# A new order for projection and router, 19 ring slots with six early weight halves, and a pool for the memory keys that closes with attention

## The chip, the cores and the metric

The kernel runs on one NeuronCore of a Trainium2 chip. The metric is the device time of one execution in microseconds; the median of three executions of the kernel before is 940.51 us (937.72 to 942.25). Engines: PE is TensorE's matmul, PEld its weight load, DVE is VectorE, ACT is ScalarE, POOL is GpSimd, SP is SyncE, which issues nearly all loads here.

## The reference

One decoder layer on 512 tokens of width 1024. Three attention branches (block-sparse, stick-breaking, and cross-attention into 256 memory tokens) share one projection; their gated sum goes through an output projection; two layer norms stand around the residual; then each token picks one of four groups and two of the eight experts in it.

```python
proj = x @ w_in
...
merged = (gates[:, :, 0] * (y_a @ w_br_moba)
          + gates[:, :, 1] * (y_b @ w_br_sb)
          + gates[:, :, 2] * (y_m @ w_br_mem))
mix = merged @ w_out
x = layer_norm(ALPHA * x + mix)          # norm 1
...
e_in_group = e_logits[top group]         # router
top_l, top_i = lax.top_k(e_in_group, 2)
gate = g_p * jax.nn.softmax(top_l)
...
h = jax.nn.silu(xb @ w_gate[e]) * (xb @ w_up[e])
y = h @ w_down[e]                        # 32 experts, 1024 -> 512 -> 1024
x = layer_norm(ALPHA * x + combined)     # norm 2
```

## The kernel before

The work runs in stages. First all projections, the attention of the three branches and the gates, with every fp32 matmul split into three rounded ones (`mm3`, L122). Then the output projection of the merged branches: its first four K-tiles are added up on the way (`add_out`), the last four are kept (`wo`, L581) and are done by `project(t)` (L824), t being one of four blocks of 128 tokens. `project` does 24 matmuls of 128x512: two column halves, K-tiles 0 to 2 first, then K-tile 3, which needs `mg[7]`, the last merged block. It adds the result to x1, norms the block (`norm`, L596) and sends it to DRAM. `turn_x` (T) transposes a normed block, `route` (L) computes router logits and the two picked experts (`ab`), `place` (R) ranks the block's tokens among all before it (`rank`) and builds the selection matrix `sel`, and `gather0` (A) gathers the block's tokens for the first pair of experts. ORDER (L48) is the list in which TensorE executes these steps; TensorE follows it to the letter, whereas VectorE, ScalarE and GpSimd are ordered by a planner that prefers, among what it holds for ready, what was emitted first.

Then 16 pairs of experts, `pair_step(p)`: gate (two halves of K), combine of the pair before, up (two halves), hidden, transposes, down (two halves of columns). A weight half is 128x2048 fp32, 1 MB; a pair has 12, there are 192. They are loaded by `fetch` (L528) into a ring of 18 slots (`ring`, L517): RB = 4 in `ring2`, which is there right after attention, RA = 9 in `ring1` (after the projections), RC = 4 in `ring3` and RD = 1 in `ring4` (after the router); two more go into a tile "once", used in pair 0 alone. A slot is allocated in a fixed rotation over the four pools, so a half waits until its pool has a slot given back. `ahead(n)` issues n halves; 4 are issued during the projections (two when ct is 2, two when ct is 4), 20 in all ahead of pair 0.

After pair 0 stands a loop with a bound known only at run time (the overflow of experts with over 64 tokens, L1158), which all engines enter and leave together. Ahead of it `ahead(BEFORE)` issues six more halves; the halves behind it can't be issued until the loop is left. The rest of the kernel runs over pairs 1 to 15, and `last` (L1108) does the last pair's down projection, the combine and norm 2, all engines in the order written. There `inner(t, i)` applies mean and gain to a block of 128x512 on VectorE, `outer(t, i)` the deviation and offset, by TensorE and ScalarE, or by VectorE for the blocks in BYDVE, and `ship` stores it.

Of the kernel before, what the change touches and what calls it, by code (L numbers as in the profile page):

```python
# [11 lines left out]
F32 = mybir.dt.float32  # L12
F32R = mybir.dt.float32r
# [4 lines left out]
ALU = mybir.AluOpType  # L18
# [4 lines left out]
P = 128  # L23
S = 512
D = 1024
KT = D // P
TT = S // P
# [6 lines left out]
WB, LOOK = 2, 1  # L34
F_M, F_A, F_B = 3.9, 3.9, 3.9
H = (slice(0, 64), slice(64, 128))
RA, RB, RC, RD = 9, 4, 4, 1
HALF = 2048
MIDP = 0
BEFORE = 6  # L40
CW = 184
BIG = 8192.0
XTB = 2
HTB = 1
BYDVE = ((3, 0), (3, 1))
BANKS = ("ht", "gu", "dn", "cb", "xgp", "cb", "", "")
FIRST = (2, 1)
ORDER = "G0 G1 T0 G2 L0 T1 G30 L1 R0 G31 A0 T2 L2 T3 R1 L3 R2 A1 R3 A2 A3"  # L48


@with_exitstack
def layer(ctx, tc, xT, xn, memT, w_qk, w_v, w_mk, w_mv, w_g, w_o, rb, oh, ln, wr, br,
# [34 lines left out]
    astk = ExitStack()  # L87
# [2 lines left out]
    xl = xp.tile([P, KT, S], F32R, name="xl")  # L90
    yh = yp.tile([P, KT, S], F32R, name="yh")
    yl = yp.tile([P, KT, S], F32R, name="yl")
    vm = xp.tile([P, 2, 256], F32, name="vm")
    km = [[xp.tile([P, 256], F32R, name=f"km{i}{j}") for j in range(2)] for i in range(2)]
    identb = cpool.tile([P, P], BF16, name="identb")
    ve.tensor_copy(identb, ident)
    maskb = cpool.tile([P, P], BF16, name="maskb")
# [24 lines left out]
    def mm3(o, pairs, start=True, stop=True):  # L122
        n = len(pairs)
        for i, (lh, ll, rh, rl) in enumerate(pairs):
            pe.matmul(o, lh, rh, start=start and i == 0, stop=False)  # L125
            pe.matmul(o, ll, rh, start=False, stop=False)  # L126
            pe.matmul(o, lh, rl, start=False, stop=stop and i == n - 1)  # L127
# [421 lines left out]

    todo = [x for p in range(16) for x in pieces_of(p)]  # L550

    todo[4:15] = todo[4:6] + todo[8:15] + todo[6:8]
    taken = [0]

    def ahead(n, ts=()):

        for i in range(n):
            e, j, c = todo[taken[0]]
            taken[0] += 1
            pieces[e, j, c] = fetch(e, j, c, ts[i] if i < len(ts) else None)  # L560
# [5 lines left out]
    for ct in range(6):  # L566
        jobs.finish(f"br{ct}")
        if ct == 3:
            lastw[0] = jobs.last
            for i in range(2):  # L570
                after(nc.sync.dma_start(lnb[:, i, :], ln[i:i + 1, :].to_broadcast([P, D])), lastw[0])
            after(nc.sync.dma_start(wrt, wr), lastw[0])
            after(nc.sync.dma_start(brt, br.to_broadcast([P, 40])), lastw[0])
        if ct in (2, 4):
            lastw[0] = jobs.last
            ahead(2)
    jobs.finish("g23")
    jobs.load(len(jobs.jobs) - 1)
    xstk.close()
# [7 lines left out]
    def bank3(tag):  # L587
        return ps.tile([P, 512], F32, name=tag, tag=tag, bufs={"gu": 2, "dn": 2, "xgp": 1, "ht": 1, "cb": 2}[tag])
# [1 line left out]
    half = cpool.tile([P, 1], F32, name="half")  # L590
    ve.memset(half, -0.5)

    rw = op.tile([P, TT, 96], F32, name="rw")
    sm = op.tile([P, TT, 8], F32, name="sm")

    def norm(t, sm, gb, sp):  # L596
# [18 lines left out]
    rpool = ctx.enter_context(pool("rout", waits="tile"))  # L615
    gpool2 = ctx.enter_context(pool("slots", waits="tile"))

    cs = rpool.tile([P, CW], F32, name="cs")
    nc.sync.dma_start(cs, cst[:, 0:CW])
    nc.sync.dma_start(cs2, cst[:, CW:CW + 160])  # L620
# [200 lines left out]
    pairs[0].start()  # L821
    first = []

    def project(t, cols=(0, 1)):  # L824

        ts = slice(t * P, (t + 1) * P)
        os_ = [bank3("dn") for c in cols]
        for ks in (range(3), range(3, 4)):
            for c, o in zip(cols, os_):
                r = slice(c * 512, (c + 1) * 512)  # L830
                mm3(o, [(mg[4 + k][0][:, ts], mg[4 + k][1][:, ts], wo[k][0][:, r], wo[k][1][:, r]) for k in ks],
                    start=ks[0] == 0, stop=ks[0] == 3)
        for c, o in zip(cols, os_):
            r = slice(c * 512, (c + 1) * 512)
            ve.scalar_tensor_tensor(out=x1[:, t, r], in0=x1[:, t, r], scalar=1.0, in1=o, op0=ALU.mult, op1=ALU.add,
                                    accum_out=sm[:, t, c:c + 1])
        if 1 in cols:
            norm(t, sm, lnb, op)
            gp.dma_start(xdr[ts, :], x1[:, t, :])
# [10 lines left out]
    with tc.manual_schedule(engines={mybir.EngineType.PE}):  # L850
        xt_ = {}
        for step in ORDER.split():
            t = int(step[1])
            if step[0] == "G":
                project(t, (0, 1) if len(step) == 2 else (int(step[2]),))
                if t == 0:
                    first += [bank3("xgp"), bank3("cb")]
            elif step[0] == "T":
                xt_[t] = turn_x(t)
            elif step[0] == "L":  # L860
                route(t, xt_[t])
            elif step[0] == "R":
                place(t)
            else:
                gather0(t)
        settle()
# [179 lines left out]
    def last_norm(gb):  # L1046

        col = lambda i: slice(i * 512, (i + 1) * 512)

        def inner(t, i):  # L1050
            x = x1[:, t, col(i)]
            ve.scalar_tensor_tensor(out=x, in0=x, scalar=sm2[:, t, 5:6], in1=gb[:, 0, col(i)], op0=ALU.add, op1=ALU.mult)  # L1052

        def ship(t, i):
            nc.sync.dma_start(out[t * P:(t + 1) * P, col(i)], x1[:, t, col(i)])

        m, d = sm2[:, :, 5], sm2[:, :, 6]
        ve.tensor_tensor(out=m, in0=sm2[:, :, 0], in1=sm2[:, :, 1], op=ALU.add)
        ve.tensor_scalar(out=m, in0=m, scalar1=-1.0 / D, scalar2=None, op0=ALU.mult)
        ve.scalar_tensor_tensor(out=d, in0=sm2[:, :, 0], scalar=2.0 / D, in1=m, op0=ALU.mult, op1=ALU.add)  # L1060
        ve.tensor_tensor(out=d, in0=d, in1=d, op=ALU.mult)
        inner(0, 0)

        v = [sm2[:, :, i] for i in range(8)]
        ve.scalar_tensor_tensor(out=v[3], in0=v[3], scalar=EPS * D ** 3 / 4.0, in1=v[4], op0=ALU.add, op1=ALU.add)
        ve.scalar_tensor_tensor(out=v[3], in0=v[3], scalar=4.0 / D ** 3, in1=v[6], op0=ALU.mult, op1=ALU.subtract)
        gp.tensor_tensor(out=v[7], in0=v[3], in1=half.to_broadcast([P, TT]), op=ALU.pow)
        inner(0, 1)
        inner(1, 0)
        diag = late[0].tile([P, TT, P], F32, name="diag", tag="hT", bufs=1)  # L1070

        def spread(ts):
            ve.tensor_tensor(out=diag[:, ts, :], in0=ident.unsqueeze(1).to_broadcast([P, ts.stop - ts.start, P]),
                             in1=v[7][:, ts].unsqueeze(2).to_broadcast([P, ts.stop - ts.start, P]), op=ALU.mult)

        def outer(t, i):
            x = x1[:, t, col(i)]
            if (t, i) in BYDVE:
                ve.scalar_tensor_tensor(out=x, in0=x, scalar=v[7][:, t:t + 1], in1=gb[:, 1, col(i)], op0=ALU.mult, op1=ALU.add)
            else:  # L1080
                pe.matmul(os_[t, i], diag[:, t, :], x, start=False, stop=True)  # L1081
                sc.copy(x, os_[t, i])
            ship(t, i)

        inner(1, 1)
        spread(slice(0, 2))
        for t in range(2):
            outer(t, 0)
            outer(t, 1)
        inner(2, 0)  # L1090
        spread(slice(2, 4))
        outer(2, 0)
        inner(2, 1)
        outer(2, 1)
        inner(3, 0)
        inner(3, 1)
        outer(3, 0)
        outer(3, 1)

    os_ = {}  # L1100

    def offset(gb, a, b):

        for n in range(a, b):
            os_[n // 2, n % 2] = o = bank3(BANKS[n])
            pe.matmul(o, ident, gb[:, 1, n % 2 * 512:n % 2 * 512 + 512], start=True, stop=False)

    def last(hT):  # L1108
        pair = pairs[15]
        b = [None, None]  # L1110

        def part(c, ks):
            if ks[0] == 0:
                pair.room(c)
                b[c] = bank3("dn")
                held[:] = [weights(30 + q, 2, c) for q in range(2)]
            for k in ks:
                for q in range(2):
                    pe.matmul(b[c][H[q]], hT[:, k, H[q]], held[q][:, k * 512:(k + 1) * 512], start=k == 0, stop=k == 3)  # L1119

        part(0, range(4))
        pair.out = b[0]
        pair.finish(0)
        part(1, range(2))
        lnt = ring().rearrange("p (a b) -> p a b", b=D)
        for i in range(2):
            nc.sync.dma_start(lnt[:, i, :], ln[2 + i:3 + i, :].to_broadcast([P, D]))
        last_sums(0, ("cb", "xgp", "gu", "cb"))
        part(1, range(2, 4))
        ve.tensor_copy(pair.y_h[1], b[1])  # L1130
        ve.tensor_tensor(out=pair.y_l[1], in0=b[1], in1=pair.y_h[1].bitcast(F32), op=ALU.subtract)
        offset(lnt, 0, 2)
        last_sums(1, ("cb", "xgp", "gu", "cb"))
        offset(lnt, 2, 6)
        last_norm(lnt)

    hTs = []
# [20 lines left out]
    with tc.For_i(0, nov, 1) as i:  # L1158
# [13 lines left out]
        ve.tensor_copy(pair.si[0:64, 0:1], sp[0:64, 0:1])  # L1172
        ve.tensor_copy(pair.si[0:64, 2:3], sp[0:64, 1:2])
        pair.rows(64)
        pair.xg = late[0].tile([P, KT, 64], F32, name="xg_o")
        o = bank3("xgp")
        for k in range(KT):
            pe.transpose(o[:, k * 64:(k + 1) * 64], xrow[0][0:64, k * P:(k + 1) * P], ident[0:64, 0:64])
# [120 lines left out]
```

## Time and profile before

| | us |
|---|---|
| median of three executions | 940.51 |
| the profiled execution, its own time | 942.12 |
| its span, first to last instruction | 940.3 |
| PE busy | 896.4 (95%) |
| DVE busy | 454.3 (48%) |
| ACT busy | 261.8 (28%) |
| DMA, mean rate over the span | 272 GB/s, 255.58 MB |

Busy time of TensorE counts from a matmul's issue to its modelled end, so a busy TensorE isn't one at its peak. The granted clock of TensorE is given as a share of full speed: 1.00 is 2.4 GHz, 0.50 is 1.2 GHz; its mean is 0.992. Times in the rows are from the span's start.

### The profile page before, as it was taken

To read this page: it belongs to the slowest core of one execution; us is meant where nothing else is said; L and a number is where in the kernel's file an instruction comes from. 1 tells how busy PE (TensorE), PEld (TensorE's weight loads), DVE (VectorE), ACT (ScalarE), POOL (GpSimd) and SP (SyncE) were. 2 spreads that over 40 slices of the span, in tenths; PEclk is the share of its full clock that TensorE was granted. 3 is DMA by queue.
4 is the path that set the end of the run, shared out by engine and by line. 5 is a ranking of instruction groups with operands and counts; after the bars stand their busy time and mean duration, and the time that the engine had idled before them with its cause. 6 is when DMAs were issued, how large, how long until landed. Compare 5 with 4: busy or idle time off the path is not lost. (4 is left out here: it accounts for less than half of the span.)

```text
span 940.3 us, 11698 instructions
## 1 busy us (share of the span) xinstructions
PE 896.4 (95%) x4444; PEld 554.5 (59%) x4444; DVE 454.3 (48%) x1050; ACT 261.8 (28%) x498; POOL 42.5 (5%) x40
## 2 busy tenths in 40 slices
PE   6999999999999999999989999999999999999996
PEld 6788888777688888878624444344443334334433
DVE  5776776665764553277454324243332234212226
ACT  6465564554422223323311111011110011001104
POOL 2000000000000000042000000000000000000000
PEclk9999999999999999999999999999999999999999
DMA  8233241221344432289869999999999999999982
GB/s 290 93 112 114 70 144 68 68 68 68 135 183 143 184 108 90 90 319 365 329 248 410 422 421 419 420 419 421 419 421 420 419 420 420 421 421 420 420 363 90
DMA packets 46946, 255.58 MB, mean 272 GB/s; under 512 B 6958, under 2 KB 8149, under 8 KB 22440
## 3 DMA queue, kind: packets, MB, share of 16 engines
q1 hardware_dynamic: 42480, 247.84, 66.7%
q0 software_dynamic: 2736, 6.11, 1.7%
q10 hardware_dynamic: 1672, 0.85, 0.3%
q8 instruction: 36, 0.59, 0.3%
q14 instruction: 22, 0.18, 0.1%
HBM read 254.43 MB, written 4.20 MB: 275 GB/s over the span
## 5 line engine op out<-in xcount | busy, mean ns | idle before, releaser
L955 PE MATMUL gu<-r,xg 128*64 128x512 f32 x1008 | 238.5, 599 | 13.4 <-DMA r<-in_we_dram 12.6
L955 PEld LDWEIGHTS gu<-r,xg 128*64 128x64 f32 x1008 | 78.6, 137 | 160.6 <-issue 131.6
L104 DVE TENSOR_TENSOR wl<-wraw,wh 128x1024 fp32r<-128x1024 f32 (+2 forms) x71 | 81.0, 1144 | 88.6 <-ACT wh L103 88.5
L125 PE MATMUL pj<-xh,wh 128*128 128x512 f32 x304 | 120.6, 397 | 0.0
L126 PE MATMUL pj<-xh,wl 128*128 128x512 f32 x304 | 118.6, 390 | 1.1 <-DVE wl L104 1.1
L127 PE MATMUL pj<-xl,wh 128*128 128x512 f32 x304 | 118.7, 391 | 0.0
L982 PE MATMUL dn<-r,hT 128*64 128x512 f32 x480 | 109.4, 598 | 5.4 <-ACT hT L972 5.4
L103 ACT CAST wh<-wraw 128x1024 fp32r<-128x1024 f32 (+2 forms) x71 | 70.3, 990 | 80.5 <-PE z L127 23.4
L803 DVE TENSOR_TENSOR x<-x,cb 128x512 f32<-128x512 f32 x60 | 38.4, 681 | 110.2 <-PE cb L801 110.2
L982 PEld LDWEIGHTS dn<-r,hT 128*64 128x64 f32 x480 | 31.9, 136 | 61.4 <-issue 52.1
L125 PEld LDWEIGHTS pj<-xh,wh 128*128 128x128 f32 x304 | 57.0, 188 | 14.4 <-issue 2.1
L126 PEld LDWEIGHTS pj<-xh,wl 128*128 128x128 f32 x304 | 57.1, 188 | 12.8 <-DVE wl L104 1.4
L127 PEld LDWEIGHTS pj<-xl,wh 128*128 128x128 f32 x304 | 57.1, 188 | 12.1
L964 DVE SCALAR_TENSOR_TENSOR u<-gu,si,g 128x512 f32<-128x512 f32 x16 | 12.0, 751 | 101.8 <-PE gu L955 96.7
L766 ACT COPY xg<-xgp 128x512 f32<-128x512 f32 x15 | 8.8, 587 | 160.5 <-PE xgp L765 160.5
L103 ACT CAST y_h<-dn 128x512 fp32r<-128x512 f32 x31 | 18.2, 586 | 100.8 <-PE dn L982 97.0
L963 ACT ACTIVATE g<-gu 128x512 f32<-128x512 f32 x16 | 9.6, 599 | 123.0 <-PE gu L955 123.0
L386 ACT ACTIVATE gt<-pj 128x512 f32<-128x512 f32 x24 | 14.4, 598 | 89.9 <-PE pj L127 89.9
L803 DVE TENSOR_TENSOR x<-x,dn 128x512 f32<-128x512 f32 x60 | 38.3, 679 | 0.0
L104 DVE TENSOR_TENSOR y_l<-dn,y_h 128x512 fp32r<-128x512 f32 x31 | 21.3, 688 | 33.0 <-ACT y_h L103 32.9
L755 POOL DMA_INDIRECT xrow<-xdr,ix x15 | 14.9, 994 | 398.9 <-DVE sel L732 316.3
L800 PE MATMUL cb<-y_h,sT 128*128 128x512 f32 x64 | 28.7, 448 | 0.0
(636 smaller groups left out, 1310.3 us busy)
## 6 DMA issues: line engine op xcount, KB each, us to landing
r<-in_we_dram SPq DMA_DIRECT2D x189, 1024.0 KB, 20.2
wraw<-in_w_g_dram SPq DMA_DIRECT2D x32, 512.0 KB, 3.3
wraw<-in_w_qk_dram SPq DMA_DIRECT2D x14, 512.0 KB, 3.3
wraw<-in_w_v_dram SPq DMA_DIRECT2D x16, 384.0 KB, 3.3
wraw<-in_w_o_dram SPq DMA_DIRECT2D x8, 512.0 KB, 3.3
xraw<-in_xT_dram SPq DMA_DIRECT2D x4, 512.0 KB, 7.9
x<-in_xn_dram SPq DMA_DIRECT2D x4, 512.0 KB, 5.6
xdr<-x POOLq DMA_DIRECT2D x4, 512.0 KB, 8.6
```

Source lines behind the costliest of these rows:

```text
L103: sc.copy(dst_h, src)
L104: (gp if eng is gp else ve).tensor_tensor(out=dst_l, in0=src, in1=dst_h.bitcast(F32), op=ALU.subtract)
L125: pe.matmul(o, lh, rh, start=start and i == 0, stop=False)
L126: pe.matmul(o, ll, rh, start=False, stop=False)
L127: pe.matmul(o, lh, rl, start=False, stop=stop and i == n - 1)
L386: after(sc.activation(out=t, in_=o, func=AF.Sigmoid), last_exp[0])
L755: gp.indirect_dma_start(xrow[0][0:n], None, xdr, bass.IndirectOffsetOnAxis(ap=ix[0:n, 0:1], axis=0), bounds_check=S - 1, oob_is_err=False)
L800: pe.matmul(o, sT, self.y_h[c][0:n], start=True, stop=False)
L803: ve.tensor_tensor(out=x1[:, t, r], in0=x1[:, t, r], in1=o, op=ALU.add)
L955: pe.matmul(o[H[q]], pairs[p].xg[:, k, H[q]], held[q][:, k % 4 * 512:k % 4 * 512 + 512], start=k == 0, stop=k == KT - 1)
L964: ve.scalar_tensor_tensor(out=hs, in0=u, scalar=pairs[p].si[:, 0:1], in1=gs, op0=ALU.mult, op1=ALU.mult)
L982: pe.matmul(o[H[q]], hT[:, k, H[q]], w[q][:, k * 512:(k + 1) * 512], start=k == 0, stop=k == 3)
```

## The change

Constants: RA 9 to 8 and RB 4 to 6, so 19 ring slots, of which six can be loaded early (three when ct is 2, three when ct is 4), and 21 halves are issued ahead of pair 0; BEFORE 6 to 7. `project` can be cut into K-tiles 0 to 2 (P) and K-tile 3 (Q); the two halves of block 1 use the banks "ht" and "cb" instead of "dn". ORDER is new. In `last_norm` block (2, 1) joins those done by VectorE, the offsets use five banks instead of six, and the stores are issued behind everything else in the order SHIP. The memory keys and values (`km`, `vm`) get a pool that closes with attention; `rw` moves from the pool `outp` to `rout`; the overflow loop's tile `xg_o` shares a tag.

```diff
-RA, RB, RC, RD = 9, 4, 4, 1
+RA, RB, RC, RD = 8, 6, 4, 1
...
-BEFORE = 6
+BEFORE = 7
...
-BYDVE = ((3, 0), (3, 1))
-BANKS = ("ht", "gu", "dn", "cb", "xgp", "cb", "", "")
+SHIP = ((0, 0), (0, 1), (2, 1), (1, 0), (3, 0), (1, 1), (3, 1), (2, 0))
+BYDVE = ((2, 1), (3, 0), (3, 1))
+BANKS = ("ht", "gu", "dn", "cb", "xgp")
 FIRST = (2, 1)
-ORDER = "G0 G1 T0 G2 L0 T1 G30 L1 R0 G31 A0 T2 L2 T3 R1 L3 R2 A1 R3 A2 A3"
+ORDER = "P0 P1 Q0 P2 Q1 T0 Q2 G30 L0 T1 G31 L1 R0 A0 T2 R1 A1 L2 T3 R2 A2 L3 R3 A3"
...
-    vm = xp.tile([P, 2, 256], F32, name="vm")
-    km = [[xp.tile([P, 256], F32R, name=f"km{i}{j}") for j in range(2)] for i in range(2)]
+    kmp = astk.enter_context(pool("kmp"))
+    vm = kmp.tile([P, 2, 256], F32, name="vm")
+    km = [[kmp.tile([P, 256], F32R, name=f"km{i}{j}") for j in range(2)] for i in range(2)]
...
-    todo[4:15] = todo[4:6] + todo[8:15] + todo[6:8]
+    todo[RB:RA + RB + 2] = todo[8:RA + RB + 2] + todo[RB:8]
...
-            ahead(2)
+            ahead(RB // 2)
...
-    rw = op.tile([P, TT, 96], F32, name="rw")
...
+    rw = rpool.tile([P, TT, 96], F32, name="rw")
...
-    def project(t, cols=(0, 1)):
+    parts = {}
+    def project(t, cols=(0, 1), ks=range(4)):
         ts = slice(t * P, (t + 1) * P)
-        os_ = [bank3("dn") for c in cols]
-        for ks in (range(3), range(3, 4)):
-            for c, o in zip(cols, os_):
+        for c in cols:
+            if (t, c) not in parts:
+                parts[t, c] = bank3(("ht", "cb")[c] if t == 1 else "dn")
+        for kk in (range(3), range(3, 4)):
+            for c in cols:
                 r = slice(c * 512, (c + 1) * 512)
-                mm3(o, [(mg[4 + k][0][:, ts], mg[4 + k][1][:, ts], wo[k][0][:, r], wo[k][1][:, r]) for k in ks],
-                    start=ks[0] == 0, stop=ks[0] == 3)
+                if kk[0] in ks:
+                    mm3(parts[t, c], [(mg[4 + k][0][:, ts], mg[4 + k][1][:, ts], wo[k][0][:, r], wo[k][1][:, r]) for k in kk],
+                        start=kk[0] == 0, stop=kk[0] == 3)
+        if 3 not in ks:
+            return
...
-                if t == 0:
+                if t == 3 and len(first) == 0:
                     first += [bank3("xgp"), bank3("cb")]
+            elif step[0] in "PQ":
+                project(t, ks=range(3) if step[0] == "P" else range(3, 4))
...
-            ship(t, i)
...
-        inner(2, 1)
-        outer(2, 1)
-        inner(3, 0)
-        inner(3, 1)
-        outer(3, 0)
-        outer(3, 1)
+        for t, i in ((2, 1), (3, 0), (3, 1)):
+            inner(t, i)
+            outer(t, i)
+        for t, i in SHIP:
+            ship(t, i)
...
-        offset(lnt, 2, 6)
+        offset(lnt, 2, 5)
...
-        pair.xg = late[0].tile([P, KT, 64], F32, name="xg_o")
+        pair.xg = late[0].tile([P, KT, 64], F32, name="xg_o", tag="sq", bufs=1)
```

## Rows read from the trace of the kernel before

**Rows 1.** Page: busy tenths of the span in 40 equal slices.

```profile
PE   6999999999999999999989999999999999999996
...
DMA  8233241221344432289869999999999999999982
```

**Rows 2.** Stretch: us, busy us (x) of PE, PEld, DVE, ACT, POOL, PEclk, DMA share, GB/s.

```profile
430.00:437.50 7.50, 7.50 (x46) 6.50 (x45) 7.19 (x35) 1.91 (x4) 1.57 (x2) 1.00 0.92 379
...
478.20:484.50 6.30, 4.22 (x22) 1.46 (x20) 2.84 (x19) 1.93 (x4) 0.00 (x0) 1.00 0.01 1
484.50:586.80 102.30, 101.31 (x479) 42.27 (x480) 39.69 (x106) 11.11 (x21) 3.96 (x4) 0.98 1.00 410
586.80:895.00 308.20, 291.81 (x1335) 120.92 (x1333) 97.49 (x238) 35.58 (x65) 9.86 (x10) 1.00 1.01 420
```

**Rows 3.** Chain that ended last: start us, us, what.

```profile
874.35 20.59 DMA r<-in_we_dram
...
894.98 3.65 PE gu L955 x14
```

**Rows 4.** Issues of L534 until 484.5: count, duration ns min/median/max, first and last start.

```profile
L534 SPq DMA_DIRECT2D r<-in_we_dram x24: 327/400/440, 262.4 to 469.3; - x24
```

**Rows 5.** PE in time, projection's start: start us, us, what, [idle before <-releaser].

```profile
406.39 0.39 PE L125 MATMUL dn<-woh,mgh 128*128 128x512 f32 x1
406.62 0.39 PE L126 MATMUL dn<-woh,mgl 128*128 128x512 f32 x1
...
411.99 0.49 PE L125 MATMUL dn<-woh,mgh 128*128 128x512 f32 x1 [1.33 <-ACT mgh L103]
412.71 0.50 PE L126 MATMUL dn<-woh,mgl 128*128 128x512 f32 x1 [0.23 <-DVE mgl L104]
```

**Rows 6.** PE in time, router: A0's first half, T2, L2, L3, pair 0's gate.

```profile
437.35 1.06 PE L843 MATMUL xgp<-sel,x 128*128 128x128 f32 x8
...
439.13 1.04 PE L648 MATMUL gu<-ident,x 128*128 128x128 f32 x8
441.30 1.98 PE L656 MATMUL cb<-wrt,xt 128*128 128x40 f32 x16 [1.13 <-ACT xt L649]
...
444.47 3.63 PE L656 MATMUL cb<-wrt,xt 128*128 128x40 f32 x16
...
455.94 7.09 PE L955 MATMUL gu<-r,xg 128*64 128x512 f32 x32 [0.77 <-ACT xg L869]
```

**Rows 7.** Two stretches, columns as in rows 2: the granted clock.

```profile
413.20:416.60 3.40, 3.40 (x10) 2.58 (x9) 1.66 (x6) 0.75 (x1) 0.00 (x0) 0.50 1.01 426
...
443.90:450.70 6.80, 6.72 (x38) 6.55 (x37) 4.68 (x39) 1.08 (x2) 0.00 (x0) 0.50 0.99 373
```

**Rows 8.** DVE in time: norm of block 2, route 0, rank 0, selection 0, route 2's end.

```profile
432.71 1.41 DVE L610 SCALAR_TENSOR_TENSOR x<-x,sm,lnb 128x512 f32<-128x512 f32 x2
434.04 0.24 DVE L671 SCALAR_TENSOR_TENSOR ab<-cs,ix,oh 128x32 bf16<-128x32 f32 x1
...
434.91 0.18 DVE L684 TENSOR_TENSOR rw<-ht,cs 128x32 f32<-128x32 f32 x1
...
436.07 0.35 DVE L733 SCALAR_TENSOR_TENSOR sel<-cs,dst,sel 128x128 f32<-128x128 f32 x1
...
445.75 0.24 DVE L671 SCALAR_TENSOR_TENSOR ab<-cs,ix,oh 128x32 bf16<-128x32 f32 x1
```

**Rows 9.** SP in time: the fifth and the seventh half issued behind the loop.

```profile
490.19 0.33 SPq L534 DMA_DIRECT2D r<-in_we_dram  x1
...
499.24 0.33 SPq L534 DMA_DIRECT2D r<-in_we_dram  x1
```

**Rows 10.** DMA issues at 437.5: count, size, us from issue to landing.

```profile
r<-in_we_dram SPq DMA_DIRECT2D x1, 1024.0 KB, 5.1
```

**Rows 11.** DVE and SP in time, the end: VectorE's last two blocks, the last store.

```profile
932.38 1.41 DVE L1079 SCALAR_TENSOR_TENSOR x<-x,sm,r 128x512 f32<-128x512 f32 x2
...
936.51 0.41 SPq L1055 DMA_DIRECT2D out_dram<-x  x1
```

More of the change, by code (lines that the diff above doesn't have):

```diff
@@ L822, in layer @@
     first = []
-    def project(t, cols=(0, 1)):
+    parts = {}
+    def project(t, cols=(0, 1), ks=range(4)):
         ts = slice(t * P, (t + 1) * P)
-        os_ = [bank3("dn") for c in cols]
-        for ks in (range(3), range(3, 4)):
-            for c, o in zip(cols, os_):
-                r = slice(c * 512, (c + 1) * 512)
-                mm3(o, [(mg[4 + k][0][:, ts], mg[4 + k][1][:, ts], wo[k][0][:, r], wo[k][1][:, r]) for k in ks],
-                    start=ks[0] == 0, stop=ks[0] == 3)
-        for c, o in zip(cols, os_):
+        for c in cols:
[3 more added lines that the diff above has]
+            for c in cols:
+                r = slice(c * 512, (c + 1) * 512)
+                if kk[0] in ks:
[3 more added lines that the diff above has]
+            return
+        for c in cols:
             r = slice(c * 512, (c + 1) * 512)
-            ve.scalar_tensor_tensor(out=x1[:, t, r], in0=x1[:, t, r], scalar=1.0, in1=o, op0=ALU.mult, op1=ALU.add,
+            ve.scalar_tensor_tensor(out=x1[:, t, r], in0=x1[:, t, r], scalar=1.0, in1=parts[t, c], op0=ALU.mult, op1=ALU.add,
                                     accum_out=sm[:, t, c:c + 1])
```

## The prediction

> **What bounds the kernel now.** I read the busy slices first, then a table by stage, then the chain that ended last, and then the stage before the chain begins. The slices show two halves: until the 17th the DMA engines are mostly idle while TensorE stands at 9 from the second on, and from the 22nd they are full [rows 1]. The table puts numbers on it: from 484.5 us on the core draws 410 to 420 GB/s at a DMA share of 1.00 to 1.01 [rows 2]. An expert half is 128x2048 fp32, 1.0486 MB, so it takes 2.50 us at 420 GB/s. The chain agrees: until 895 us it hops from one weight transfer to the next, 20.6 us per hop, and from 894.98 TensorE carries it to the end [rows 3]. So the end follows one sum: the time at which the transfers run without a pause, plus the halves still missing times 2.5 us, plus a tail. The pause before that time is the runtime loop (the overflow loop): at 478.2:484.5 the DMA share is 0.01 [rows 2]. By then 24 ring halves and 2 in the "once" tile have been issued [rows 4], 26 of 192.
>
> The loop is left 28.6 us after U, the first gate matmul of pair 0 (455.94 to 484.5) [rows 2, 6]. Nothing between hangs on the router, so a later U is a later end, microsecond for microsecond. U itself is set by projection and router, 406.4 to 455.9, in which TensorE executes a list written out by hand.
>
> The profiled execution took 942.12 us (span 940.3); the median of the three runs is 940.51. I make the sum against the former and shift it by -1.6.
>
> **Part one: projection, 406.4 to the end of G31.** A G of both column halves is 24 matmuls; one costs 0.23 (406.39 to 406.62) [rows 5]. Before, G0's last quarter waits 1.33 us for mg[7], and the granted clock then falls to 0.50 (1.2 instead of 2.4 GHz) for 413.2:416.6 [rows 5, 7]. In the new order P0 and P1 (36 matmuls, 8.2 us) stand ahead of that quarter, until 414.6, past the readiness of mg[7] at 412.7 [rows 5]; wait and slow clock go. The new work until G31 ends is 96 matmuls (21.9 us), T0 and T1 (0.9 each: a gather's two groups of eight take 1.78, 437.35 to 439.13 [rows 6], and a T is one such group) and L0 (1.7: route 2's 1.98 without its drain [rows 6]), 25.4 us, plus some 0.5 for banks that VectorE has to empty (P2 needs the "dn" banks of P0): 432.3. Before it ended at 437.35, where A0 begins [rows 6]. That is 5 us earlier, but L1 and R0 (1.9 us) have only been moved behind it.
>
> **Part two: the router's tail.** Before, other work stands between a rank (R) and the gather (A) that needs its selection: R0 G31 A0, R1 L3 R2 A1. In the new list each A stands right behind its R, and TensorE executes in order, so the wait is bare. From R's matmul to the finished selection takes 1.6 us (L684 at 434.91 to L733's end at 436.42) [rows 8]; from L's last matmul to the finished ab 2.7 us (L2's end 443.28 to 445.99) [rows 6, 8]. With A at 1.8 us, T 0.9, L 1.7, the new tail is at least: 432.3, L1 434.0, R0 434.2, +1.7, A0 437.7, T2 438.6, R1, +1.9, A1 442.4, L2 444.1, +2.7 (T3 hides in it), R2 447.0, +1.6, A2 450.4, L3 452.1, +2.7, R3 455.0, +1.6, first half of A3 457.5, copy of xg 0.8 (the 0.77 that it left TensorE idle before [rows 6]): U = 458.3, 2.4 us later than before. This is the floor.
>
> Two things come on top. First, VectorE is nearly full there: 7.19 of 7.50 us in 430:437.5 [rows 2]. It takes what was emitted first: route 0's last operation (L671) stands at 434.04 behind L610 of block 2's norm [rows 8]. In the new list G31, with its norm, comes ahead of L1 and R0. That norm runs some 5.3 us (432.3 to 437.6, with 1.4 us of ScalarE inside), so rank 0's selection is ready at about 439.5 and A0 starts at 439.6, not 435.9. The chain behind it shifts by these 3.7: U = 462.0, +6.1.
>
> Second, the granted clock. In 443.9:450.7 it was 0.50 [rows 7], after a stretch in which TensorE had 1.13 us of idle and then small matmuls (route 3 took 3.63 us, route 2 1.98) [rows 6]. The new tail has five waits of 1.6 to 2.7 us and one of 5. The matmuls on its chain from A0 to A3 sum to 10.6 us at full clock; all of it at 1.2 GHz costs 10.6 more, none of it 0. Before, with one such gap, 6.8 of the 18.6 us from A0 to U were slow, 37%; with six I take half, 5.3. U = 467.3, +11.4; ends +2.4 and +16.7.
>
> [...]
>
> **Part three: 19 slots and a seventh half before the loop.** The early halves become six (three at ct 2, three at ct 4), ring1 one fewer; 21 instead of 20 are issued ahead of pair 0, and 7 instead of 6 between U and the loop. So 28 instead of 26 are in hand at the loop's exit: 2 x 2.50 = 5.0 us less to load. The third early half costs SyncE one issue of 0.4 us and the next weight tile of the projection up to 2.5 us of queueing, twice; I put it at nothing, because TensorE stays at 9 in all slices of that stage, in which both pairs are loaded (the first at 262.4) [rows 1, 4], with three raw buffers ahead of it; uncovered it costs 2.5 each. The seventh half waits for a slot that pair 0's first down projection gives back (about 22 us after U) and blocks SyncE until then; behind it on that queue stands only the load of the loop's bound, and the loop waits for TensorE anyway. It lands 5.1 us after its issue if nothing is queued [rows 10], within the pause at 478.2:484.5, so it is free.
>
> Not all 5.0 arrives. After the loop, pair 0's ten ring slots less those refilled are free: four before, three now. The next come with pair 1's gate, 5.7 us after the exit (490.19), and then only at 14.7 (499.24) [rows 9]. Before, six transfers bridge that: the first lands 5.1 after its issue [rows 10], the sixth at 5.1 + 5 x 2.5 = 17.6, and the seventh is due at 20.1 and can land at 14.7 + 5.1 = 19.8: no pause. Now five bridge it, the sixth is due at 17.6 and lands at 19.8: 2.2 lost. Later slots come in pairs in the same way and may cost a little more. I take 2.3 of 5.0 as lost: -2.7; ends -5.0 (the queue never dries) and -1.7 (a second pause of 1.0). The Trainium skill (DMA: Bandwidth & Descriptors, Specifications) gives about 358 GB/s from HBM per core; a half would cost 2.93 us by it and the two would be worth 5.9. The trace's 420 GB/s decides here.
>
> **Part four: the end.** Block (2,1) moves from TensorE and ScalarE to VectorE, and the stores leave in the order of SHIP. Before, VectorE's last two blocks are done at 933.79 but are stored behind ScalarE's sixth, the last at 936.51 [rows 11]. Now VectorE runs three inner and three outer steps of 0.69 to 0.78 from 930.4 to about 934.9, ScalarE, one block short, ends with (2,0) some 0.9 earlier than with (2,1), and the last store is issued at about 935.4: -1.1 (ends -0.9 and -1.4). One bank offset fewer (two matmuls) hides under ScalarE's squares.
>
> **Nothing:** rw in another pool, the memory keys and values in a pool closed with attention, the overflow tile's tag. They add no instruction; the loop body is emitted and not executed. What they could cost is a wait for a reused address, which would show as idle of TensorE behind attention.
>
> **Sum.** +6.1 (order) +5.3 (clock) -2.7 (halves) -1.1 (end) = +7.6: 949.7 against the profiled execution, 948.1 as a median.
>
> **Rivals.** (1) The clock stays up, or recovers within each gather: +2.3, 942.8 us. For it: at 450.7 it came back while the tail was still running [rows 7]. Against it: two falls after smaller gaps than the new ones [rows 5 to 7]. (2) Faster: the order costs almost nothing. VectorE, five us ahead of its old schedule, has rank 0 ready in time, the bare latencies shrink to those of uninterleaved chains (route 2.3 instead of 2.7, twice), U = 457.5, +1.6; with the whole 5.0 and 1.4 it is -4.8, 935.7. It decides for "faster" from U at or below 457.5. Against it: VectorE's 7.19 of 7.50 [rows 2]. (3) The lead of two halves isn't one: the seventh's slot is only given back by the second down projection, the loop starts some 2 us later, and the empty queue behind the loop eats the rest: +7.6 +2.7 +2.0 = +12.3, 952.8.
>
> **How the numbers follow.** Forecast 0.50 (948.1, its own range 944 to 953), rival 1 0.28, rival 2 0.10, rival 3 0.12. A measurement of this kernel can tell about 0.5% from no change, 4.7 us: faster is below 935.8, slower above 945.2. Slower: 0.45 of the forecast and rival 3, 0.57; same: rival 1 and 0.05, 0.33; faster: 0.10. The range reaches from above rival 2 to just above rival 3: 938 to 953.5.
>
> **What would show it.** Right: idle of TensorE ahead of A0, A1, A2, A3 with VectorE named; a granted clock of 0.5 over a good part of 437 to 465; U at 463 to 470 and the loop left 28.6 us later; 28 halves issued before it, three right behind it, and a DMA share under 1 some 15 us after; the last store 1.1 us earlier against the last norm. Wrong: U at 458 or earlier, or a loop that is left more than 28.6 us after U.

## The result, and the profile after

The changed kernel takes 950.9 us as a median (947.75 to 951.93), the kernel before 940.25 beside it (937.72 to 942.25): a ratio of 1.0109, 95% interval 1.0075 to 1.0143. It is slower by 1.1%, 2.8 us above the 948.1 of the forecast and inside its range. The profiled execution took 947.75 us (span 945.9, mean granted clock 0.990); the other three had 0.986 to 0.987.

The table by stage of after has the columns of [rows 2]. The first row answers 430:437.5 there. Rows two to four are the new stretches at half clock, which answer [rows 7]; then come the loop's pause, the first 102 us behind it, and the rest.

```profile
430.00:437.50 7.50, 4.04 (x28) 3.42 (x26) 6.57 (x29) 1.31 (x3) 3.08 (x4) 0.91 0.85 297
436.10:442.90 6.80, 3.05 (x14) 3.06 (x15) 3.69 (x13) 0.00 (x0) 1.52 (x2) 0.50 1.00 398
453.20:456.60 3.40, 2.89 (x13) 2.89 (x14) 0.42 (x2) 0.00 (x0) 0.00 (x0) 0.50 0.00 0
460.00:466.80 6.80, 3.96 (x19) 3.56 (x20) 5.27 (x31) 2.09 (x3) 0.00 (x0) 0.50 0.13 24
489.00:495.30 6.30, 4.24 (x23) 1.48 (x20) 2.87 (x19) 1.95 (x4) 0.00 (x0) 1.00 0.53 168
495.40:597.70 102.30, 100.94 (x486) 42.72 (x488) 40.53 (x107) 12.17 (x22) 3.96 (x4) 1.00 1.00 407
597.70:901.00 303.30, 289.70 (x1328) 117.42 (x1324) 96.78 (x236) 34.52 (x62) 9.85 (x10) 1.00 1.01 420
```

In 430:437.5 TensorE is now busy for 4.04 of 7.50 us, where it was full in [rows 2]. Its waits are the next view, TensorE in order of time, only the instructions that it idled ahead of (the idle time and who ended it stand in brackets), and pair 0's first gate, U:

```profile
434.89 0.18 PE L684 MATMUL ht<-ab,trib 128*128 128x32 bf16 x1 [1.03 <-DVE ab L673]
439.85 2.08 PE L852 MATMUL xgp<-sel,x 128*128 128x128 f32 x8 [4.78 <-DVE sel L735]
445.85 1.16 PE L852 MATMUL xgp<-sel,x 128*128 128x128 f32 x8 [1.56 <-DVE sel L735]
451.98 0.18 PE L684 MATMUL ht<-ab,trib 128*128 128x32 bf16 x1 [1.40 <-DVE ab L673]
453.71 2.08 PE L852 MATMUL xgp<-sel,x 128*128 128x128 f32 x8 [1.56 <-DVE sel L735]
461.20 0.19 PE L684 MATMUL ht<-ab,trib 128*128 128x32 bf16 x1 [2.28 <-DVE ab L673]
463.02 2.08 PE L852 MATMUL xgp<-sel,x 128*128 128x128 f32 x8 [1.64 <-DVE sel L735]
466.74 1.53 PE L966 MATMUL gu<-r,xg 128*64 128x512 f32 x6
```

Up to the last row, which is U, these are R0, A0, A1, R2, A2, R3 and A3: 14.25 us of bare waits, all for VectorE. Before, [rows 6] had 1.13 us ahead of L2 and 0.77 ahead of U. The wait for mg[7] of [rows 5] is gone, and the projection's last matmul now starts at 431.74. VectorE says why A0 waits longest. Here are the norm of block 3, then the last two steps of rank 0's selection, which [rows 8] had at 436.07:

```profile
435.88 1.41 DVE L607 SCALAR_TENSOR_TENSOR x<-x,sm,lnb 128x512 f32<-128x512 f32 x2
437.20 1.41 DVE L611 SCALAR_TENSOR_TENSOR x<-x,sm,lnb 128x512 f32<-128x512 f32 x2
...
438.80 0.28 DVE L734 TENSOR_SCALAR sel<-cs,dst 128x128 f32<-128x128 f32 x1
...
439.45 0.34 DVE L735 SCALAR_TENSOR_TENSOR sel<-cs,dst,sel 128x128 f32<-128x128 f32 x1
```

Now the weights. First the issues of the fetch line until 495.3, in the columns of [rows 4] (26 ring halves and 2 of the "once" tile, against 24 and 2). Then SyncE in order of time, as in [rows 9]: the seventh half ahead of the loop, the three right behind it, and the fourth and the sixth behind it, which had to wait for a slot:

```profile
L536 SPq DMA_DIRECT2D r<-in_we_dram x26: 327/410/697, 261.8 to 488.7; - x26
...
L536 SPq DMA_DIRECT2D once<-in_we_dram x2: 328/386/444, 438.6 to 439.0; - x2
```

```profile
488.66 0.33 SPq L536 DMA_DIRECT2D r<-in_we_dram  x1
...
495.38 1.28 SPq L536 DMA_DIRECT2D r<-in_we_dram  x3
...
499.31 0.33 SPq L536 DMA_DIRECT2D r<-in_we_dram  x1
...
508.39 0.33 SPq L536 DMA_DIRECT2D r<-in_we_dram  x1
```

The loop is left at 495.38, 28.64 behind U, as it was 28.6 behind it before. The seventh half went through in the pause ahead of that: 168 GB/s over the 6.30 us of 489:495.3, 1.06 MB. The chain that ended last still hops along the weights, and TensorE takes over at 900.97 instead of 894.98 [rows 3]:

```profile
880.20 20.73 DMA r<-in_we_dram
900.97 3.65 PE gu L966 x14
```

The last half lands at 920.88, 6.07 later than before (914.81), though the loop is left 10.84 later. VectorE's last step and the last two stores answer [rows 11]:

```profile
940.05 0.75 DVE L1090 SCALAR_TENSOR_TENSOR x<-x,sm,r 128x512 f32<-128x512 f32 x1
```

```profile
940.83 1.53 SPq L1066 DMA_DIRECT2D out_dram<-x  x2
```

The last store is issued at 941.73, 20.85 behind the last half (21.70 before), and takes 2.9 us to land (2.5 before). The two profiled executions thus differ by +10.8 (loop left later), -4.8 (last half against the exit) and -0.5 (from the last half to the end of the span): +5.5, where their times differ by 947.75 - 942.12 = 5.6.

### The profile page after: what moved, and what is told of

It reads as the page before. It is cut to its first block, busy times and chain, and to the rows that moved or that the text cites. A ratio compares the mean times of both kernels' runs of the same rounds, so it can differ in the third digit from the quotient of the medians.

```text
span 945.9 us, 11682 instructions
## 1 busy us (share of the span) xinstructions
PE 893.2 (94%) x4440; PEld 551.2 (58%) x4440; DVE 456.2 (48%) x1051; ACT 261.5 (28%) x497; POOL 43.1 (5%) x40
## 5 line engine op out<-in xcount | busy, mean ns | idle before, releaser
L966 PE MATMUL gu<-r,xg 128*64 128x512 f32 x1008 | 236.1, 596 | 10.2 <-DMA r<-in_we_dram 10.2
L966 PEld LDWEIGHTS gu<-r,xg 128*64 128x64 f32 x1008 | 75.5, 137 | 158.1 <-issue 134.5
L106 DVE TENSOR_TENSOR y_l<-dn,y_h 128x512 fp32r<-128x512 f32 x31 | 21.3, 689 | 32.9 <-ACT y_h L105 32.9
L757 POOL DMA_INDIRECT xrow<-xdr,ix x15 | 14.9, 993 | 409.0 <-DVE sel L734 311.8
```

The source lines that it names most:

```text
L106: (gp if eng is gp else ve).tensor_tensor(out=dst_l, in0=src, in1=dst_h.bitcast(F32), op=ALU.subtract)
L757: gp.indirect_dma_start(xrow[0][0:n], None, xdr, bass.IndirectOffsetOnAxis(ap=ix[0:n, 0:1], axis=0), bounds_check=S - 1, oob_is_err=False)
L966: pe.matmul(o[H[q]], pairs[p].xg[:, k, H[q]], held[q][:, k % 4 * 512:k % 4 * 512 + 512], start=k == 0, stop=k == KT - 1)
```

## The experiments

The profiled executions start the projection at different times (405.3 to 407.8 us), so the router is compared by its path: from the projection's first matmul to U. It is 49.55 us before (406.39 to 455.94) and 60.97 after (405.77 to 466.74). The sets of executions were taken on different chips, each with executions of the kernel before beside them, so medians of different sets are compared by their ratio to it.

**The old order back.** Only the list is undone, so slots, seventh half and end are as changed.

```diff
-ORDER = "P0 P1 Q0 P2 Q1 T0 Q2 G30 L0 T1 G31 L1 R0 A0 T2 R1 A1 L2 T3 R2 A2 L3 R3 A3"
+ORDER = "G0 G1 T0 G2 L0 T1 G30 L1 R0 G31 A0 T2 L2 T3 R1 L3 R2 A1 R3 A2 A3"
```

> The changed kernel with one line undone: ORDER is the old one; slots, seventh half and end stay as changed. Theory (the new order costs the time, the halves and the end give some back): pair 0's first gate (U) back at 455 to 457 us, the loop left 28.6 behind it, 28 halves issued by then; the halves give 2.7 to 4.8 and the end 0.5 to 1.1, so 934 to 937 us as a median, 3 to 6 less than the kernel before. Rival A (the two halves in hand are no lead, the empty queue behind the loop eats it): 939 to 941. Rival B (the slots or the seventh half cause the loss, not the order): 947 or more.

> e1_old_order once more, beside the kernel with fillers, on the same chip and in more rounds: 932 to 937 as a median, with single executions up to 940 where the granted clock falls in the router (e7_six_before, with the same router, took 933.7 to 939.9). Theory: U at 450 to 451 where the clock stays up, at 454 to 457 where it falls.

Measured: 933.85 us, ratio 0.9927 (0.9906 to 0.9948), and in the second set, on another chip, 936.41 (932.79 to 940.67), ratio 0.9963 (0.9943 to 0.9984). So the order is the loss and the rest a gain; rival B is out. The path was shorter than I expected: U at 450.34 and 450.26, 44.95 and 44.94 us, with the granted clock at 1.00 all along it, though the waits ahead of G0's last quarter (1.25) and of L2 (1.13) are nearly those of [rows 5, 6]. So, by this comparison, 4.6 of the 49.55 us before were slow clock, which the order doesn't bring about each time. A profile of the old order with six halves ahead of the loop (below) bears that out: it holds 10.2 us at half clock, as before does, and its path is 48.97, 4.0 longer. Behind the loop there is the pause that the prediction had put into after. First SyncE in order of time: three halves right behind the exit, then the fourth and the sixth. Then the first 3 us behind the exit and a stretch 14.5 to 17.5 us behind it, columns as in [rows 2]:

```profile
478.98 1.28 SPq L536 DMA_DIRECT2D r<-in_we_dram  x3
...
484.73 0.33 SPq L536 DMA_DIRECT2D r<-in_we_dram  x1
...
493.78 0.33 SPq L536 DMA_DIRECT2D r<-in_we_dram  x1
```

```profile
478.98:481.98 3.00, 2.90 (x10) 0.93 (x12) 1.64 (x8) 0.00 (x0) 0.00 (x0) 0.56 0.65 194
...
493.50:496.50 3.00, 3.00 (x16) 1.00 (x14) 0.00 (x0) 0.00 (x0) 0.00 (x0) 1.00 0.63 186
```

Pair 1 begins at a clock of 0.56 here, as it did at half clock in the trace before, and its slots come 14.8 us behind the exit. In after pair 1 ran at 1.00 and they came at 13.0, and the DMA share 14.5 to 17.5 us behind the exit was 0.96. The other runs with 28 halves in hand fall apart in the same way: the six profiles in which pair 1 began with half clock have 0.61 to 0.70 there, the five at full clock 0.92 to 1.00.

**The new order alone.** The kernel before, with the new list and the code that cuts `project`.

```diff
-ORDER = "G0 G1 T0 G2 L0 T1 G30 L1 R0 G31 A0 T2 L2 T3 R1 L3 R2 A1 R3 A2 A3"
+ORDER = "P0 P1 Q0 P2 Q1 T0 Q2 G30 L0 T1 G31 L1 R0 A0 T2 R1 A1 L2 T3 R2 A2 L3 R3 A3"
...
```

> The kernel before with the new ORDER alone (and the code that cuts project into K-tiles 0 to 2 and K-tile 3); 18 slots, six halves ahead of the loop, the old end. Theory: U at 466 to 468, granted clock 0.5 over some 17 us of 436 to 467, the loop left at 495, six transfers behind it: 10 to 12 more than before in the profiled execution, 950 to 953 as a median; with a clock below full speed later on, up to 956. Rival B (the order isn't the cause): 939 to 943.

Measured: 954.77 us, ratio 1.0141 (1.0121 to 1.0161); U at 469.57, a path of 62.78. The waits ahead of A0, A1, R2 and A2 are those of after to the hundredth (4.78, 1.56, 1.40, 1.56); R3's is 2.26 and A3's 1.64. U comes 13.63 later than before and the span is 13.5 longer, with the same slots and the same end: here a microsecond of U is a microsecond of time. Against after only the clock is low for longer, in 23.8 instead of 17 us (the last 1.8 of them behind U):

```profile
437.00:443.40 6.40, 2.54 (x12) 2.54 (x13) 3.81 (x13) 0.00 (x0) 1.56 (x2) 0.50 1.00 408
454.00:471.40 17.40, 12.89 (x59) 11.24 (x61) 6.83 (x39) 5.97 (x7) 0.00 (x0) 0.51 0.15 48
```

**Fillers in the waits.** To part the clock from the waits, work that nobody needs was put into them. The first two tries chose its operands badly.

```diff
+ORDER = "P0 P1 Q0 P2 Q1 T0 Q2 G30 L0 T1 G31 L1 F4 R0 F9 F9 A0 T2 R1 F6 A1 L2 T3 F5 R2 F6 A2 L3 F9 R3 F6 A3"
...
+            elif step[0] == "F":
+                o = bank3("dn")
+                for i in range(t):
+                    pe.matmul(o, mg[4][0][:, 0:P], wo[0][0][:, 0:512], start=i == 0, stop=i == t - 1)
```

> The changed kernel with 54 matmuls of 128x512 on old operands put into the waits of the new order (4 ahead of R0, 18 ahead of A0, 6, 5, 6, 9 and 6 ahead of A1, R2, A2, R3 and A3), a little shorter than each wait; their results are read by nobody. They add work that the reference doesn't have. Theory (a good part of the cost is the granted clock, which falls behind the waits): the granted clock is 1.00 over most of 436 to 465, the waits that are left are under 0.6 each, U comes 4 to 6 us earlier, at 461 to 463, and the time is 943 to 947. Rival 1 (the clock costs nothing on this path, the waits alone do): U stays at 466 to 468 and the time at 950 to 952. Rival C (the fillers are longer than the waits and push the gathers): U above 468.

Measured: 957.44 us. The router did nearly what the theory said: the granted clock was 1.00 from the projection to U, and U came at 463.16, though A0 still waited 1.80 where under 0.6 was expected. The loss came from elsewhere. TensorE at A0, at U and behind the loop, then the next half on SyncE:

```profile
440.74 0.49 PE L852 MATMUL xgp<-sel,x 128*128 128x128 f32 x2 [1.80 <-DVE sel L735]
...
463.16 0.65 PE L970 MATMUL gu<-r,xg 128*64 128x512 f32 x2
...
500.80 0.27 PE L747 MATMUL xgp<-gmb,sel 128*128 128x9 bf16 x4 [11.15 <-DMA r<-in_we_dram]
```

```profile
460.96 0.33 SPq L536 DMA_DIRECT2D r<-in_we_dram  x1
```

That half goes out at 431.93 in after, right behind the start of the projection's last matmul (431.74). The fillers read `wo` until 460.9, a ring slot takes over that address, and seven halves, this one the first, went out between 460.96 and 464.5. TensorE then stood 11.15 us at the loop, for a weight transfer by the profile, where it stands 2.1 to 2.2 in every other run, and the loop was left at 500.80.

> The changed kernel with 58 matmuls of 128x512 in the waits of its router, as in e3_filler, but reading the identity and a weight half of pair 0 that has been there since 268 us, so that no slot is held longer for them (in e3_filler they read wo, whose address a ring slot takes over: the next half went out at 460.96 instead of 431.93 us, and the loop was left 37.6 instead of 28.6 us behind U). They add work that the reference doesn't have, and their results are read by nobody. Theory (half the cost of the tail beyond the waits is the granted clock): U at 462 to 464 with the granted clock at 1.00 from 436 on, the loop left 28.6 behind it, 944 to 947. Rival 1 (the clock costs nothing on this path): U at 466 to 468, 949 to 952.

Measured: 979.91 us. Here the operands held nothing up, but a 128x512 filler of plain fp32 operands took 0.87 us (38 records, two to a matmul, in 16.47 us) against the 0.23 of [rows 5], where the operands are rounded: U at 496.66. The third try used small bf16 matmuls.

```diff
+ORDER = "P0 P1 Q0 P2 Q1 T0 Q2 G30 L0 T1 G31 L1 F2 R0 F12 A0 T2 R1 F4 A1 L2 T3 F3 R2 F4 A2 L3 F6 R3 F4 A3"
...
+            elif step[0] == "F":
+                o = bank3("dn")
+                for i in range(6 * int(step[1:])):
+                    pe.matmul(o[:, 0:P], identb, identb, start=i == 0, stop=i == 6 * int(step[1:]) - 1)
```

> The changed kernel with 210 bf16 matmuls of 128x128 (identity times identity, into a bank that nobody reads) in the waits of its router: 12 ahead of R0, 72 ahead of A0, 24, 18, 24, 36 and 24 ahead of A1, R2, A2, R3 and A3, a little shorter than each wait at about 0.055 each. They add work that the reference doesn't have and hold no slot and no weight. (In e5_filler_w the fillers were of fp32 operands and took 0.9 each, so that U came at 496.66 and the time was 979.91.) Theory (half of what the tail costs beyond the waits is the granted clock): clock 1.00 over most of 436 to 465, U at 461.5 to 463.5 as in e3_filler, the loop left 28.6 behind it, 28 halves by then, 943 to 948. Rival 1 (the clock costs nothing on this path): U at 466 to 468, 949 to 952. Rival H (such small matmuls don't hold the clock up): stretches of 0.50 stay, U at 465 or later, 948 or more.

Measured: 946.04 us (943.64 to 946.84), ratio 1.0056 (1.0039 to 1.0073). The stretch from R0 to U, and TensorE at A0 and at U:

```profile
434.60:462.00 27.40, 25.21 (x325) 24.20 (x326) 15.31 (x87) 9.33 (x13) 1.56 (x2) 1.00 0.61 250
```

```profile
439.50 1.16 PE L852 MATMUL xgp<-sel,x 128*128 128x128 f32 x8 [0.75 <-DVE sel L735]
...
461.91 4.51 PE L970 MATMUL gu<-r,xg 128*64 128x512 f32 x20
```

The granted clock is 1.00, the path is 56.46 us, 4.5 shorter than in after, and the median is 4.9 lower, although TensorE has 210 matmuls more. VectorE takes as long as in after: from R0 to A0 it is 4.96 us in both, from R1 to A1 1.74 and 1.73; the waits are only filled. So the clock cost 4.5 us, and the other part of the loss is the waits. Rivals 1 and H are out.

**Fillers in the old order.** The same, 18, 18 and 12 of them, ahead of G0's last quarter, L2 and R3.

> e1_old_order with such bf16 fillers in its three waits: 18 ahead of the last quarter of G0, 18 ahead of L2, 12 ahead of R3. Theory (the old order's bare chain gives U at 450.3 and the rest is the clock): the granted clock stays at 1.00 from 405 to 450, U at 450 to 451, 931 to 935 in every execution. Rival H (fillers of this size don't hold the clock up): U up to 456, 933 to 940, as with the old order alone.

Measured: 933.28 us (932.19 to 935.30), ratio 0.9932 (0.9908 to 0.9957), against 936.41 (932.79 to 940.67) without fillers on the same chip. The stretch from A0 to U, and U:

```profile
434.80:450.40 15.60, 15.23 (x155) 14.76 (x153) 12.51 (x72) 8.63 (x13) 2.52 (x3) 1.00 0.94 368
```

```profile
450.47 1.08 PE L974 MATMUL gu<-r,xg 128*64 128x512 f32 x4
```

The path is 44.95 us, as in both profiles of the old order whose clock stayed up; what the fillers take away is the spread. Against the first set of the old order (933.85, ratio 0.9927) there is no gain to be told. This version beats both kernels. Beside the one above it gives the price of the order at full clock: 56.46 against 44.95, 11.5 us.

**One half fewer ahead of the loop.** The old order again, with BEFORE back at 6.

> e1_old_order with BEFORE back at 6: 19 slots and six early halves stay, the seventh half goes out behind the loop. It tells what one half in hand is worth. Theory (the queue hardly dries, a half in hand is worth nearly its 2.5): 27 halves by the loop's exit, four right behind it, the last half lands 1.9 to 2.5 later against the loop's exit than in e1_old_order (426.6 behind it), 935 to 937. Rival F (an empty queue behind the loop eats the seventh half, as the prediction's 2.3 of 5.0 has it): under 0.5 later, 933 to 935.

Measured: 936.34 us, ratio 0.9951 (0.9929 to 0.9973): its ratio lies between the 0.9927 and the 0.9963 of the two sets with seven. The last half's issue, in us from the loop's exit, says how much the halves in hand are worth, once pair 1's clock is kept apart:

| halves by the exit | pair 1 at half clock first | pair 1 at full clock |
|---|---|---|
| 26 | 412.9 (before) | 411.7 (new order alone) |
| 27 | | 409.1 (this one) |
| 28 | 409.0 to 409.4 in six profiles (old order 409.2) | 407.4 to 408.8 in five (after 408.05, bf16 fillers in old and new order 407.4 and 408.8) |

At full clock the first half of the two brings its full 2.6; the seventh ahead of the loop 0.3 to 1.7. There is one profile each with 26 and with 27 halves at full clock, and they differ in their list too, so these are estimates. Rival F holds for the seventh in part.

**Other lists.** Three of the following keep the cut of the projection without the new tail, and one moves rank 0 (with L0 and L1) alone.

```diff
+ORDER = "P0 P1 Q0 Q1 P2 T0 Q2 L0 T1 G30 L1 R0 G31 T2 L2 A0 R1 T3 L3 R2 A1 R3 A2 A3"
```

> The changed kernel with another ORDER: P0 P1 Q0 Q1 P2 T0 Q2 L0 T1 G30 L1 R0 G31 T2 L2 A0 R1 T3 L3 R2 A1 R3 A2 A3. The cut of the projection that closes the wait for mg[7] stays; between each rank and its gather other work stands again. Theory (the loss is the gather right behind its rank, the cut itself is a gain): R0 is done before G31, whose 12 matmuls hide its selection; no wait ahead of A0 over 0.5, waits of 1 to 2 us only ahead of R2, A2 and A3; U at 451 to 455, 930 to 935 us, less than with the old order. Rival D (VectorE is full there, so that the selections are late in any order): U at 456 to 460, 936 to 941. Rival B (the order isn't the cause): 948 or more.

Measured: 933.48 us (930.01 to 938.87), ratio 0.9931 (0.9901 to 0.9961). A0 doesn't wait; T3 waits 1.43, and U is at 453.24, with 6.8 us at half clock on the way (442.3 to 449.1). It is faster than both kernels, by as much as the old order is.

```diff
+ORDER = "P0 P1 Q0 Q1 T0 G2 L0 T1 G30 L1 R0 G31 A0 T2 L2 T3 R1 L3 R2 A1 R3 A2 A3"
```

> The changed kernel with the cut of the projection (P0 P1 Q0 Q1, then block 2 whole) and behind it the old list word for word, so with other work between each rank and its gather. Theory (the cut is a gain, the tail is the loss): no wait ahead of Q0, the projection ends 1.2 to 1.5 earlier than in e1_old_order, U at 448.5 to 450 at full clock (450.34 in e1_old_order), up to 455 if the clock falls in the router; 930 to 934 as a median. Rival E (the cut gains nothing, since VectorE's norms set the tail's pace): U at 450 or later at full clock, 933 to 936. Rival B (the order isn't the cause): 947 or more.

Measured: 939.08 us, ratio 0.9981 (0.9960 to 1.0001). My expectation missed what covers the norm of block 0, which T0 needs: in the old list all of G1 stands between that block's last matmul and T0, here only the six matmuls of Q1, since P1 has moved ahead of Q0. TensorE stood 3.79 ahead of T0 (the row names no releaser; VectorE's last step of that norm starts at 419.90):

```profile
420.74 1.30 PE L650 MATMUL gu<-ident,x 128*128 128x128 f32 x8 [3.79 <-issue]
```

```diff
+ORDER = "P0 P1 Q0 P2 Q1 T0 L0 Q2 T1 G30 L1 R0 G31 A0 T2 R1 A1 L2 T3 R2 A2 L3 R3 A3"
```

> The changed kernel with L0, L1 and R0 moved ahead: ORDER is P0 P1 Q0 P2 Q1 T0 L0 Q2 T1 G30 L1 R0 G31 A0 T2 R1 A1 L2 T3 R2 A2 L3 R3 A3. From A0 on it is the new list; what is gone is the norm of block 3 ahead of rank 0 on VectorE. Theory (that backlog is 3.7 us of U, the waits ahead of A1, R2, A2, R3 and A3 stay): A0 waits under 0.5 instead of 4.8, U at 460 to 464 with a clock that still falls, 943 to 948. Rival G (the norms only move, and T3, R2 or R3 waits longer for them): A0 starts early and U stays at 465 to 468, 948 to 951.

Measured: 950.15 us, ratio 1.0097 (1.0065 to 1.0129); U at 468.62. Rank 0 is now ahead of G31, but T1 waits 1.71 for a norm, the projection ends 6 us later, and A0 still waits 2.10, starting at 440.36 instead of 439.85. The theory's gain of 3.7 didn't come. VectorE shows why, with the addition of block 3's projection (L844) and the last step of rank 0's selection:

```profile
438.29 0.69 DVE L844 SCALAR_TENSOR_TENSOR x<-x,dn 128x512 f32<-128x512 f32 x1 [2.21 <-PE dn L129]
...
439.95 0.35 DVE L735 SCALAR_TENSOR_TENSOR sel<-cs,dst,sel 128x128 f32<-128x128 f32 x1
```

The norm of block 3 no longer stands ahead of the selection, but the addition that it begins with does: VectorE takes it up first and idles 2.21 us until G31 ends, with rank 0's last steps behind it.

The last one has the cut with cover ahead of T0, the old list from A0 on, and the bf16 fillers.

```diff
+ORDER = "P0 P1 Q0 Q1 P2 T0 Q2 L0 T1 G30 L1 R0 G31 A0 T2 F3 L2 T3 R1 L3 R2 A1 F2 R3 A2 A3"
```

> The cut of the projection with cover, and the old list from A0 on: ORDER is P0 P1 Q0 Q1 P2 T0 Q2 L0 T1 G30 L1 R0 G31 A0 T2 L2 T3 R1 L3 R2 A1 R3 A2 A3, with 18 bf16 fillers ahead of L2 and 12 ahead of R3 as in e10_old_filler. In e6_cut_alone T0 waited 3.79 for the norm of block 0, because P1 stood ahead of Q0 and only Q1 behind it; here P2 stands there too. Theory (the cut takes away the wait for mg[7], and behind it VectorE's norms set the pace): no wait ahead of Q0, T0 waits under 0.5, G31 ends some 0.9 earlier than in e10_old_filler, T3 waits for block 3's norm, U at 449.5 to 450.5, 931.5 to 934.5, not to be told from e10_old_filler (933.28). Rival I (the cut is worth the wait that it takes away): U at 449.2 or earlier, 930 to 932.

Measured: 935.57 us (932.60 to 940.32), ratio 0.9946 (0.9924 to 0.9968): above the expected 931.5 to 934.5, and by its ratio not to be told from the 0.9932 of the old order with fillers. TensorE's waits at A0 and A1, and the stretch behind A1:

```profile
436.39 1.16 PE L852 MATMUL xgp<-sel,x 128*128 128x128 f32 x8 [1.15 <-DVE sel L735]
...
446.29 1.54 PE L852 MATMUL xgp<-sel,x 128*128 128x128 f32 x8 [0.94 <-DVE sel L735]
```

```profile
446.60:450.60 4.00, 4.00 (x33) 3.94 (x32) 1.79 (x16) 2.54 (x3) 0.00 (x0) 0.57 1.02 428
```

The projection takes 27.1 us to its last matmul's start instead of 29.1, but the path is 46.70, or 45.0 without the slow clock (4.00 us at 0.57, 1.7 lost), where the old order has 44.95. Two us gained by the cut come back as waits for VectorE ahead of A0 and A1. Ahead of A0 VectorE isn't full: it idles 0.82 us until 435.28 for the end of G31, again ahead of the addition of block 3 (L844), with the selection's last step (436.00) behind it. Rival I is out.

## Why the prediction was right, and where it wasn't

**The bound: right.** In every kernel above the loop is left 28.6 to 29.3 us behind U, except where the weights came late (37.6), and a microsecond of U arrives at the end (with the new order alone 13.63 us of U as 13.5 of the span).

**The order: right in size.** The prediction had U at 467.3 and a path of 60.9; the trace has 466.74 and 60.97. That they agree so closely is luck in part, since two errors cancel: without slow clock the path was to be 55.6 and is 56.46 with fillers, and the clock was to cost 5.3 and costs 4.5. The 0.9 lie ahead of A0, which comes 34.1 us behind the projection's start instead of 33.2; from A0 to U it is 22.4 us in the prediction and with fillers. The bare waits behind A0 are 1.40 to 2.28, where 1.6 to 2.7 was written. One reading was off without harm: the 1.6 us from R to its selection count from VectorE's first step (434.91), not from R's matmul (434.48), which makes it 1.9; from R1 to A1 it took 1.73 in after.

**The backlog of VectorE: seen where it was put, not shown as the cause by itself.** The norm of block 3 does stand ahead of rank 0's selection in the trace. But moving rank 0 ahead of it gained nothing, since VectorE then idled for G31 with the selection behind it. What holds is narrower: in the old order, where R0 stands ahead of G31, the selection is ready (433.76) before VectorE comes to that addition (434.88), and A0 doesn't wait for it. So the order in which VectorE takes its steps counts, as the prediction had it, but an earlier place in TensorE's list didn't bring the selection ahead of block 3's steps there.

**The clock: right in size (5.3 against 4.5), wrong in its comparison.** The prediction charged the new order with slow clock against a profile that held 10.2 us at half clock of its own [rows 7], 4.6 us of path. So the order's price at equal clock isn't +6.1 but 11.5, and the kernel before seems to have the same kind of loss in some executions and not in others: its executions have mean clocks of 0.988 to 0.998, and the longer ones have the lower clocks. This is why the medians differ by 10.65 and the two profiles by 5.6: after's profile (947.75) has the highest clock of its four executions, and before's (942.12) is at the slow end of its own. So the sum, +7.6, was 2.0 too high for the profiles and 3 too low for the medians; that the median fell 2.8 from the forecast owes something to which executions were profiled.

**Rival 1, by its condition, was half right.** With the clock up the changed kernel is still slower, 946.04 and not 942.8, as the order costs 11.5 of which the halves and the end return only part. The Trainium skill (TensorE: Matmul & The Clock Gate, the closing table on why this matters) advises against long idle gaps between bursts of matmuls, so that throughput doesn't drop mid-kernel. Here gaps of little over 1 us were followed by a drop too, but not each time: in the old order the 1.13 us ahead of L2 were followed by half clock in the profiles of before (from 443.9) and of the kernel with six halves ahead of the loop (from 442), and not in the two of the old order with seven. With the gaps filled, the profiles of both orders show no fall between the projection and U. Rival 2 is out: U came at 466.74, not at 457.5.

**The halves: the mis-sized term.** -2.7 was predicted, -4.8 measured. The step that failed is that the queue dries some 15 us behind the exit. The 14.7 us to the next slots were read from a profile in which pair 1 began at half clock (0.50 for 3.4 us from 484.9), and were carried over to after. The queue does dry where pair 1 starts that way (0.63 of DMA share in the old order's stretch, slots at 14.8); in after pair 1 ran at full clock, the slots came at 13.0 and the share stayed at 0.96. By the table above, the two halves themselves are worth 3.5 to 3.9 at half clock and 2.9 to 4.3 at full clock, and pair 1's clock another 1.2, so even at half clock the loss was put too high, at 2.3 of 5.0. Rival 3 is out: the loop isn't left later, and the lead is one.

**The end: -1.1 predicted, -0.5 measured.** The last store is issued 0.85 earlier against the last half, but takes 0.4 longer to land, which the term left out. Where the clock is full from the last half to the last store, that stretch is 20.9 to 21.3 us with the new end (three profiles) and 21.7 and 22.0 with the old one (two). The other nine profiles of the new end hold 3.4 or 6.8 us at half clock in it and take 21.9 to 23.2, no less than the old end. Whether the new end brings that fall about, by taking matmuls away from TensorE, isn't shown: only two profiles have the old end.

**Left open.** Why the granted clock fell at the start of pair 1 in some executions and not in others, after the same 2.1 us pause of TensorE, isn't settled. That the pools, tags and the third early half cost nothing was not tried alone; nothing in the runs with the old order points to a cost, and in after the projection starts no later (405.77 against 406.39).

## What to carry to other kernels

When one engine follows a list written by hand, a step that waits for another engine needs independent work between it and what it waits for; here, pulling work ahead to close one wait uncovered the next. Look also at the order in which the other engine takes its steps: one that waits there holds up those behind it, however idle that engine is. Before a difference of a few us is booked to a change, take out the slow clock that the profile of before happens to hold, by comparing stretches at the same granted clock. A transfer that is issued earlier ahead of a pause is worth its full time only if the slots behind the pause still keep the queue from drying.

## What the runs showed of the hardware

Useless work can pay: on one chip, 48 bf16 matmuls of 128x128 (0.055 us each) in three waits of the old order brought its median from 936.41 to 933.28 and the spread of its executions from 7.9 to 3.1 us (12 and 6 of them). In the new order 210 of them gave back 4.5 us of path. Gaps of the same length were followed by half clock in one execution and not in another, so this kernel has a spread that belongs to it: the same kernel came out at 933.85 in one set and 936.41 in the other. And reading an operand for longer isn't free where its address is promised to a transfer: the fillers that read `wo` delayed seven weight halves, and TensorE stood 11.15 instead of 2.2 us at the loop.
